# Hybrid encoder layer: the convolution group normalised two tiles a unit with its high parts on VectorE, and the values of two head pairs placed one unit later

## The chip, the cores and the metric

One core of a Trainium2 chip runs the whole program in one launch. The metric is the device time of one execution in microseconds (us). The kernel before takes 1961.98 us, the median of three runs (1961.77 to 1962.09).

## The reference

One encoder layer over 512 tokens of 2048 channels, in float32, cut here to what matters:

```python
xn = rms_norm(x, attn_norm_g)
u_val, u_gate, q, k, v = split(xn @ w_in)                  # 5 x 1024 columns
y_conv = silu(layer_norm(dwconv31(u_val * sigmoid(u_gate)) + b, ln_g, ln_b))   # group A
y_na   = neighbourhood_attention(q, k, v, rpb)             # group B: 16 heads of 64, 8 x 16 window
mixed  = concat(rms_norm(y_conv, conv_out_g), rms_norm(y_na, na_out_g))
x = x + mixed @ w_out
up = dwconv3(rms_norm(x, ffn_norm_g) @ w_up)               # 2 x 5632 columns
gate, val = split(up)
x = x + (silu(gate) * val) @ w_down
return rms_norm(x, final_norm_g)
```

The change touches the LayerNorm, swish and closing norm of group A, and the step of group B in which the softmaxed scores are multiplied by the values.

## The kernel before, in words

Channels lie on the 128 partitions, tokens on the free axis; a tile is 128 x 512. Float32 products are made from two parts: an operand is split into a rounded high part and a low part that is the rest, and a product is high by high, high by low and low by high. Weights come in units of 128 x 1024, each with one DMA on SyncE's queue (`raw`), one ScalarE copy that makes the high part (`whi`, line 129) and one VectorE subtraction that makes the low part (`wlo`, line 130). `group` (lines 146 to 149) spends 24 matmuls on one unit: 16 with the high part, then 8 with the low part. `AHEAD` has the parts of three later units made while a unit is multiplied; `whi` and `wlo` have four buffers each, so the parts of unit n+4 can be made once unit n has been multiplied.

The text counts these units from the start of the program. `ORDER` gives the order of the projections. For head pair p (1 to 7) the q projection takes units 44+4p and 45+4p, the k projection units 46+4p and 47+4p; pair 6 has units 68 to 71, pair 7 units 72 to 75. Units 76 to 91 are the half of the output projection that reads group A (`out_half(ma, read_a)`), units 92 to 107 the half that reads group B.

After the last matmul of each unit `tick` lets two lists of generators take one step each: `steps` holds `attention()` (later `norm_b()`), `asteps` holds `group_a()`. What a step traces on TensorE is kept behind that matmul; work of the other engines is only ordered by its place in the program, by data and by buffers. When a step of `attention` yields a true value, `group_a` is passed over in that unit. A planner turns the traced program into one fixed order for each engine. It gives earlier instructions precedence; `shifted` moves the place at which an instruction counts (the copies of line 597 count 100 places sooner).

`attention()` does for each head pair p: load the bias tables (line 628); one unit later the products with the values of pair p-1 (`values`, line 608) and the scores of pair p (`scores`, line 562), `taken` for pair p-1 and `softmax` for pair p; three units after that (four for p in `LATER`) the transposes of the softmaxed scores (`turn`, line 588) and their copies to SBUF (`turned_p`, line 597, tiles `pt`), which `values` reads. The matmuls of the values, the scores and the transposes are pinned to program order among themselves. `values` writes two PSUM banks: one of tag "po" and one of tag "mm", which has three banks and also holds the sums of `project`. Those leave the bank through VectorE's product with the inverse root (line 536), which is traced behind the tick of the projection's second unit.

`group_a()` starts when the taps of the depthwise convolution are done. Its eight tiles `ys` are centred and squared in one step (lines 508 to 510) and, after three units and the inverse root (`roots_of_sums`, lines 271 to 284), normalised in one step: for each tile a VectorE product with the root (line 517), a ScalarE Silu (line 518) and `split` (line 208) into `mah` and `mal`, a ScalarE copy (line 211) and a VectorE instruction (line 212). Eight squares (lines 217, 220) and seven additions (line 221) follow in the same step. `RA_AFTER` units later the second root is made: `halved` splits the sum on ScalarE and VectorE (lines 260, 261), and one unit later two matmuls (`column_sums`, line 268) add it over the partitions.

Counted out through the generators, the two lists do this in the units that matter (a step stands behind the matmuls of its unit):

| unit | steps before |
|---|---|
| 62 | A: mean; centre and square tiles 0 to 7 |
| 64 | transposes and copies of pair 3 |
| 65 | values 3, scores 4, softmax 4 |
| 66, 67 | A: halves of the sum; column sums, root, normalise and split tiles 0 to 7, squares |
| 68 | transposes and copies of pair 4 |
| 69 | values 4, scores 5, softmax 5 |
| 73 | transposes and copies of pair 5; A: halves |
| 74 | values 5, scores 6, softmax 6 |
| 75 | A: column sums, second root |
| 78, 79 | transposes of pair 6; values 6, scores 7, softmax 7 |
| 82, 83 | transposes of pair 7; values 7, halves of group B's sum |

Tiles of 128 x 512 in SBUF come from one pool of 75 (`t2`): the parts of x, `ma`, `mb`, q, k, the scores, `pt` and all that is passing.

Of the kernel before, what the change touches and what calls it, by code (L numbers as in the profile page):

```python
# [12 lines left out]
AF = mybir.ActivationFunctionType  # L13
ALU = mybir.AluOpType
# [17 lines left out]
NC_ = CONV // P  # L32
# [29 lines left out]
ROW = 2048  # L62
ORDER = "aaaaaaVVaqaqqqqqqq"
LATER = (5, 6)
RA_AFTER = 5

PCOLS = [("g1", KD), ("dww", NC_ * CK), ("dwb", NC_), ("lng", NC_), ("lnb", NC_), ("cog", NC_),
         ("nag", NC_), ("g2", KD), ("fww", 2 * NF * 3), ("fwb", 2 * NF)]
# [9 lines left out]
def layer(ctx: ExitStack, tc: tile.TileContext, xT, xg, xn, xw, w_0, w_in, w_v, w_out, w_up, w_down, par, tab, g3, out):  # L78
    nc = tc.nc
# [16 lines left out]
    def t2(name, dt=F32):  # L96
        return tp.tile([P, S], dt, tag="t2k", name=name)
# [8 lines left out]
    def pc(name, i):  # L106
        o = POFF[name] + i
        return prm[:, o:o + 1]
# [12 lines left out]
    def raw_unit(src, n):  # L121
        raw = t4([P, U * P], "raw")
        return raw, nc.sync.dma_start(raw[:, :n], src)
# [81 lines left out]
        if job:  # L205
            open_job.append(job)

    def split(src, g, name):

        h, l = t2(name + "h", F32R), t2(name + "l", F32R)  # L210
        nc.scalar.activation(h, src, AF.Copy, scale=g)
        nc.vector.scalar_tensor_tensor(l, src, g, h.bitcast(F32), op0=ALU.mult, op1=ALU.subtract)
        return h, l

# [99 lines left out]
    for k in range(ROWS):  # L314
# [9 lines left out]
        else:  # L324
            his = [t2("weh", F32R)[:, :P], t2("weh", F32R)[:, P:n]]
            h, l = t2("xh", F32R), t2("xl", F32R)
            g = both[:, S + n:S + n + 1]
# [21 lines left out]
    for u in range(2):  # L349
        raw, i = raw_unit(w_in[1, :, u * U * P:(u + 1) * U * P], U * P)  # L350
# [8 lines left out]
    for step in ORDER:  # L359
# [5 lines left out]
        i = next(a_ if step == "a" else q_)  # L365
# [63 lines left out]
    def grid(t):  # L429
        return t.rearrange("p (r g c) -> p g r c", g=NB, r=WH)  # L430
# [4 lines left out]
    ys, ypair, gate = [], [], []  # L435
# [55 lines left out]
    ma, ra = [], []  # L491

    def group_a():
        yield
        while taps:
            yield
        acc = t2("acc")
        nc.vector.tensor_add(acc, ys[0], ys[1])
        for i in range(2, NC_):
            nc.vector.tensor_add(acc, acc, ys[i])  # L500
        two = halved(acc)
        yield
        yield
        ps = column_sums(two)
        mu = t2("mu")
        nc.vector.tensor_scalar(mu, ps, 1.0 / CONV, None, op0=ALU.mult)
        acc = t2("acc")
        for i in range(NC_):
            nc.vector.tensor_sub(ys[i], ys[i], mu)
            sum_sq(acc, ys[i], i == 0)  # L510
        yield
        yield
        yield
        r = yield from roots_of_sums(acc, CONV, "rln")
        acc = t2("acc")
        for i in range(NC_):
            nc.vector.tensor_mul(ys[i], ys[i], r)
            nc.scalar.activation(ys[i], ys[i], AF.Silu, scale=pc("lng", i), bias=pc("lnb", i))  # L518
            ma.append(split(ys[i], pc("cog", i), "ma"))
        for i in range(NC_):  # L520
            sum_sq(acc, ys[i], i == 0)
        for _ in range(RA_AFTER):
            yield

        ra.append((yield from roots_of_sums(acc, CONV, "ra")))

# [15 lines left out]
    def attention():  # L542


        def banks(name):
            two = psa.tile([P, 2, S], F32, tag="sc", name=name)
            return [two[:, j, :2 * SLOTS] for j in range(2)] + [
                psa.tile([P, 2 * SLOTS], F32, tag="tr", name=name, bufs=2) for _ in range(2)]

        def scores(q, k, quad, both, more):  # L550
            todo = [[], []]
            for i, (odd, even) in enumerate(quad):
                if even:
                    todo[i] += [(odd, 0, odd - 1, 3), (even, 3, even - 1, 3)]
                else:
                    todo[i] += [(odd, 0, odd - 1, 2), (odd, 2, 0, 2), (even, 4, even, 2)]
            order = [(1, 0), (1, 1), (0, 0), (0, 1)] if len(todo[1]) > 2 else [(0, 0), (1, 0), (0, 1), (1, 1)]
            order += [(1, 2)] * (len(todo[1]) > 2)
            for i, n in order:
                b, to, g, w = todo[i][n]  # L560
                for j, hp in enumerate(hps):
                    m = nc.tensor.matmul(both[j][hps[i], to * DH:(to + w) * DH], q[hp, b * DH:(b + 1) * DH],  # L562
                                         k[hp, g * DH:(g + w) * DH], start=True, stop=True)
                    if more or (i, n, j) != (*order[0], 0):
                        pin(m)

        def softmax(both, tb):
            soft = []
            for j in range(2):
                flat = t2("s")[:, :2 * SLOTS]  # L570
                s = flat.rearrange("p (i k) -> p i k", i=2)
                nc.vector.scalar_tensor_tensor(flat, both[j], DH ** -0.5, tb[:, j], op0=ALU.mult, op1=ALU.add)
                nm = sm.tile([P, 2], F32, tag="nm", name="nm")
                nc.vector.tensor_reduce(nm, s, axis=AX.X, op=ALU.max, negate=True)
                su = sm.tile([P, 2], F32, tag="su", name="su")
                for i in range(2):
                    nc.scalar.activation(s[:, i], s[:, i], AF.Exp, bias=nm[:, i:i + 1], accum_out=su[:, i:i + 1])
                nc.vector.reciprocal(su, su)
                for i in range(2):
                    nc.scalar.activation(s[:, i], s[:, i], AF.Copy, scale=su[:, i:i + 1])  # L580
                soft.append(flat)
            return soft

        def turn(soft, four):
            for n, (s, ps) in enumerate(zip(soft, four)):
                ps = ps.rearrange("p (h c k) -> p c h k", h=2, c=3)
                for c in range(3):
                    m = nc.tensor.transpose(ps[:, c], s[:, c * P:(c + 1) * P], ident)  # L588
                    if n or c:
                        pin(m)  # L590

        def turned_p(four):
            pts = []
            for ps in four:
                pt = t2("pt")[:, :2 * SLOTS]
                with shifted(-SOONER):
                    i = nc.scalar.activation(pt, ps, AF.Copy)
                pts.append(pt)
            copies[:] = [i]
            return pts  # L600

        def values(p, pts, po):
            v = vs[2 * p // NP_]
            cols = [slice(at, at + DH) for at in (p % (NP_ // 2) * P + j * DH for j in range(2))]
            for n, slot in enumerate(TURNS):
                for i, (g, quad, at, w, b) in enumerate(slot):
                    for j in (1, 0):
                        m = nc.tensor.matmul(po[i][hps[j], b * DH:(b + w) * DH], v[g // 2][hps[i], cols[j]],  # L608
                                             pts[2 * quad + j][hps[i], at * DH:(at + w) * DH],
                                             start=n == 0, stop=n == len(TURNS) - 1, skip_group_check=True)  # L610
                        if (n, i, j) != (0, 0, 1):
                            pin(m)

        def taken(p, po):
            ao = t2("ao")
            nc.scalar.activation(grid(ao), blocks(po[0]), AF.Copy)
            nc.vector.tensor_add(grid(ao), grid(ao), blocks(po[1]))
            mb.append(split(ao, pc("nag", p), "mb"))
            sum_sq(acc_na, ao, p == 0)

        pts = None
        for p in range(NP_ + 1):
            while len(qks) < min(p + 1, NP_):
                yield
            if p < NP_:
                tabs = [t4([P, 2, 2 * SLOTS], "tab") for _ in QUADS]
                for n, tb in enumerate(tabs):
                    nc.sync.dma_start(tb, tab[2 * p:2 * p + 2, :, n * 2 * SLOTS:(n + 1) * 2 * SLOTS]
                                      .rearrange("h p k -> p h k"))
            yield  # L630
            if p:
                po = [psa.tile([P, S], F32, tag="po", name="po"), psm.tile([P, S], F32, tag="mm", name="po")]
                values(p - 1, pts, po)
            if p < NP_:
                four = banks("sc")
                for n, quad in enumerate(QUADS):
                    scores(*qks[p], quad, four[2 * n:][:2], p or n)
            if p:
                taken(p - 1, po)
            if p == NP_:  # L640
                return
            soft = [s for n in range(2) for s in softmax(four[2 * n:][:2], tabs[n])]
            for i in range(4 if p in LATER else 3):
                yield i == 0
            four = banks("trp")
            turn(soft, four)
            pts = turned_p(four)

    p, n = -1, 0
# [522 lines left out]
```

## Time and profile before

| what | before |
|---|---|
| median of three runs | 1961.98 us |
| the profiled execution's own time | 1962.36 us |
| its span in the profile | 1960.4 us |
| TensorE (PE) busy | 1938.6 us, 99% |
| VectorE (DVE) busy | 1611.0 us, 82% |
| ScalarE (ACT) busy | 1083.8 us, 55% |
| GpSimd (POOL) busy | 226.3 us, 12% |
| mean granted TensorE clock | 0.995 |

The busy times are of one profiled execution. Matmuls are pipelined, so a busy TensorE is one that always has a matmul under way. A row of the timeline gives the start, the length, the engine, the line, the operation, tile written and tiles read, how many instructions are merged, and in brackets the idle time of the engine before them with what ended it. The list of waits gives the total, the number and the longest.

### The profile page before, as it was taken

The numbers are of one execution on the slowest core, as the hardware profiler recorded it, in microseconds if no ns is written. First come the engines' busy times: TensorE is split into PE (matmuls) and PEld (weight loads), VectorE is DVE, ScalarE is ACT, GpSimd is POOL, SyncE is SP. The second block draws the span as 40 slices with busy tenths as digits, with TensorE's granted clock in tenths as the row PEclk, the third lists the DMA queues.
The fourth block names the chain that finished last, engine by engine and source line by source line (L and its number), as shares of the span: only waits on it lengthen the run. The fifth ranks groups of instructions, "written<-read, shape, count | busy, mean of one in ns | idle before, by whom it ended". The sixth has DMA issues, their size and how long they took to land.

```text
span 1960.4 us, 27992 instructions
## 1 busy us (share of the span) xinstructions
PE 1938.6 (99%) x10327; PEld 1652.5 (84%) x10327; DVE 1611.0 (82%) x2310; ACT 1083.8 (55%) x1725; POOL 226.3 (12%) x310
## 2 busy tenths in 40 slices
PE   9999999979999999999999999999999999999998
PEld 8888888868888888888888888888888888888886
DVE  5999878975657898888888888888889898885764
ACT  7222233576526666666666666666666644554654
POOL 0111111100011111111111111111110300000000
PEclk9999999999999999999999999999999999999999
DMA  9676667767758899999999999999995967666553
GB/s 372 179 194 178 190 182 189 194 167 218 251 151 215 212 250 253 270 243 271 241 270 244 270 247 265 262 249 263 249 257 166 386 239 236 216 215 194 192 201 121
DMA packets 141529, 448.89 MB, mean 229 GB/s; under 512 B 14928, under 2 KB 27216, under 8 KB 139984
## 3 DMA queue, kind: packets, MB, share of 16 engines
q1 hardware_dynamic: 89168, 291.90, 43.1%
q0 software_dynamic: 42624, 148.92, 35.1%
q10 hardware_dynamic: 9600, 6.29, 1.1%
q8 instruction: 81, 1.33, 0.3%
q14 instruction: 56, 0.46, 0.1%
HBM read 428.17 MB, written 111.15 MB: 275 GB/s over the span
## 4 chain that ended last, share of the span: by engine, by line
PE 97%; ACT 1%; DVE 1%; issue 0%; ACTq 0%
PE pu L823 44%; PE pd L962 21%; PE pj L146 5%; PE pj L147 5%; PE pj L149 5%; PE pv L417 4%; PE po L146 3%; PE po L147 3%; PE po L149 3%; PE pj L455 1%; PE po L608 1%; PE pj L459 1%; PE sc L562 1%; PE trp L588 0%; PE trx L718 0%; ACT y L518 0%
## 5 line engine op out<-in xcount | busy, mean ns | idle before, releaser
L129 ACT ACTIVATE whi<-raw 128x1024 fp32r<-128x1024 f32 (+1 forms) x574 | 604.1, 1055 | 550.6 <-PE pd L962 116.0
L130 DVE TENSOR_TENSOR wlo<-raw,whi 128x1024 fp32r<-128x1024 f32 (+1 forms) x574 | 698.6, 1218 | 214.8 <-ACT whi L129 186.5
L823 PE MATMUL pu<-xc,whi 128*128 128x512 f32 x2464 | 593.1, 391 | 0.0
L823 PEld LDWEIGHTS pu<-xc,whi 128*128 128x128 f32 x2464 | 451.4, 188 | 86.8 <-DVE xc L711 0.4
L823 PEld LDWEIGHTS pu<-xc,wlo 128*128 128x128 f32 x2464 | 319.4, 191 | 13.7
L823 PE MATMUL pu<-xc,wlo 128*128 128x256 f32 x2464 | 324.3, 283 | 0.0
L962 PE MATMUL pd<-whi,ho 128*128 128x512 f32 x1232 | 305.1, 389 | 0.0
L962 PEld LDWEIGHTS pd<-whi,ho 128*128 128x128 f32 x1232 | 231.1, 188 | 48.7 <-DVE vl L836 0.5
L146 PE MATMUL pj<-xh,whi 128*128 128x512 f32 x464 | 182.0, 392 | 0.0
L485 DVE SCALAR_TENSOR_TENSOR y<-ch,prm,y 128x500 f32<-128x500 f32 (+14 forms) x240 | 176.9, 741 | 5.4
L147 PE MATMUL pj<-xl,whi 128*128 128x512 f32 x464 | 180.6, 389 | 0.0
L962 PE MATMUL pd<-wlo,ho 128*128 128x512 f32 x616 | 165.1, 389 | 0.0
L962 PEld LDWEIGHTS pd<-wlo,ho 128*128 128x128 f32 x616 | 115.6, 188 | 24.0
L832 ACT ACTIVATE pu<-pu 128x512 f32<-128x512 f32 x132 | 76.6, 580 | 92.0 <-PE pu L823 92.0
L772 POOL DMA_DIRECT2D raw<-in_w_up x88 | 78.6, 893 | 351.5 <-DVE wlo L130 160.8
L203 POOL DMA_DIRECT2D ws<-in_w_down x88 | 79.9, 907 | 316.7 <-DMA ws<-in_w_down 126.5
L149 PE MATMUL pj<-xh,wlo 128*128 128x512 f32 x464 | 114.6, 389 | 0.0
L146 PEld LDWEIGHTS pj<-xh,whi 128*128 128x128 f32 x464 | 87.1, 188 | 19.5 <-issue 1.6
L149 PEld LDWEIGHTS pj<-xh,wlo 128*128 128x128 f32 x464 | 87.1, 188 | 18.1
L147 PEld LDWEIGHTS pj<-xl,whi 128*128 128x128 f32 x464 | 87.1, 188 | 17.8
L200 POOL DMA_DIRECT2D ws<-ws x44 | 23.3, 530 | 317.5 <-PE pj L149 102.9
L200 POOL DMA_DIRECT2D ws<-in_w_down x44 | 23.4, 531 | 298.5 <-PE pj L149 125.9
(215 smaller groups left out, 2109.2 us busy)
## 6 DMA issues: line engine op xcount, KB each, us to landing
raw<-in_w_up SPq DMA_DIRECT2D x220, 512.0 KB, 5.9
ws<-in_w_down POOLq DMA_DIRECT2D x132, 512.0 KB, 6.5
raw<-in_w_up POOLq DMA_DIRECT2D x88, 512.0 KB, 7.4
raw<-ws SPq DMA_DIRECT2D x88, 512.0 KB, 3.3
raw<-in_w_down SPq DMA_DIRECT2D x66, 512.0 KB, 3.8
raw<-in_w_in SPq DMA_DIRECT2D x58, 512.0 KB, 5.3
ws<-ws POOLq DMA_DIRECT2D x44, 512.0 KB, 5.5
raw<-in_w_out SPq DMA_DIRECT2D x32, 512.0 KB, 4.9
```

Source lines behind the costliest of these rows:

```text
L129: i = nc.scalar.activation(hi[:, :n], raw[:, :n], AF.Copy)
L130: j = nc.vector.tensor_sub(lo[:, :n], raw[:, :n], hi[:, :n].bitcast(F32))
L146: nc.tensor.matmul(ps, hi, mh, start=first and k == 0, stop=False)
L147: nc.tensor.matmul(ps, hi, ml, start=False, stop=False)
L149: i = nc.tensor.matmul(ps, lo[:, wk * P:(wk + 1) * P], mh, start=False, stop=last and k == len(ws) - 1)
L203: nc.gpsimd.dma_start(wsum[c][k], w_down[k, {1: A21, 2: A11, 4: A11, 6: A12}[c]], accum_op=ALU.add, max_dma_last_dim=ROW)
L417: m = nc.tensor.matmul(banks[c], xs[2 * u + k][x][:, c * P:(c + 1) * P], w[l][:, k * S:(k + 1) * S], start=u == x == l == k == 0, stop=las ...
L485: nc.vector.scalar_tensor_tensor(y[:, a:b], h[:, a + j - PAD:b + j - PAD], prm[:, o:o + 1], y[:, a:b], op0=ALU.mult, op1=ALU.add)
L772: nc.gpsimd.dma_start(a[c], w_up[f, q2], accum_op=ALU.add)
L823: i = nc.tensor.matmul(ps[:, :n], part[:, k * P:(k + 1) * P], comb[c][k][:, :n], start=j == 0 and not more, stop=j == 2 * U - 1, skip_grou ...
L832: nc.scalar.activation(to, ps, AF.Copy)
L962: m = nc.tensor.matmul(ps[i], h[:, o + t * P:o + (t + 1) * P], w[:, d], start=start and not more and kind == 0 and j == 0, stop=stop and k ...
```

## The change

`group_a` yields inside its two loops over the tiles. The centring takes three tiles in each of two units and two in the third; the unit in which the root is taken stays. The normalisation takes two tiles a unit, each with its square and its addition behind its split. The wait of `RA_AFTER` units is gone; the halves of the second sum come in the unit behind the last two tiles. `split` gets a switch, with which the high part is made by VectorE's tensor_scalar, and `group_a` sets it. `attention` yields once more ahead of the tables where pair p-1 is in `SLOW`, that is for p = 5 and 6.

```diff
-RA_AFTER = 5
+SLOW = (4, 5)
...
-    def split(src, g, name):
+    def split(src, g, name, vector=False):
 
         h, l = t2(name + "h", F32R), t2(name + "l", F32R)
-        nc.scalar.activation(h, src, AF.Copy, scale=g)
+        if vector:
+            nc.vector.tensor_scalar(h, src, g, None, op0=ALU.mult)
+        else:
+            nc.scalar.activation(h, src, AF.Copy, scale=g)
         nc.vector.scalar_tensor_tensor(l, src, g, h.bitcast(F32), op0=ALU.mult, op1=ALU.subtract)
...
             nc.vector.tensor_sub(ys[i], ys[i], mu)
             sum_sq(acc, ys[i], i == 0)
-        yield
-        yield
+            if i % 3 == 2:
+                yield
         yield
         r = yield from roots_of_sums(acc, CONV, "rln")
...
-            ma.append(split(ys[i], pc("cog", i), "ma"))
-        for i in range(NC_):
+            ma.append(split(ys[i], pc("cog", i), "ma", True))
             sum_sq(acc, ys[i], i == 0)
-        for _ in range(RA_AFTER):
-            yield
+            if i % 2 == 1:
+                yield
...
             while len(qks) < min(p + 1, NP_):
                 yield
+            if p - 1 in SLOW:
+                yield
             if p < NP_:
```

With the same counting, the units become:

| unit | steps after |
|---|---|
| 62, 63, 64 | A: centre and square tiles 0 to 2; 3 to 5; 6 and 7 |
| 66, 67 | A: halves; column sums, root, tiles 0 and 1 |
| 68 | transposes and copies of pair 4; A: tiles 2 and 3 |
| 69 | A: tiles 4 and 5 |
| 70 | values 4, scores 5, softmax 5 |
| 71, 72, 73 | A: tiles 6 and 7; halves; column sums, second root |
| 74 | transposes and copies of pair 5 |
| 76 | values 5, scores 6, softmax 6 |
| 80, 81 | transposes of pair 6; values 6, scores 7, softmax 7 |
| 84, 85 | transposes of pair 7; values 7, halves of group B's sum |

## The prediction

> **What bounds the kernel now.** I read the page first, then the list of waits for TensorE, then the stretches around the one long wait, then the timelines of three engines there. The page and the waits:
>
> ```profile
> span 1960.4 us, 27992 instructions
> PE 1938.6 (99%) x10327; PEld 1652.5 (84%) x10327; DVE 1611.0 (82%) x2310; ACT 1083.8 (55%) x1725; POOL 226.3 (12%) x310
> PE po L608 <- ACT pt L597: 12.7, 1, 12.7
> PE warm L117 <- DVE ones L112: 1.1, 1, 1.1
> ```
>
> TensorE sets the time from end to end: it is idle for 1960.4 - 1938.6 = 21.8 us, and 12.7 us of that is a single wait, of the values' matmuls for the copies of the turned scores. So work moved between other engines, or among steps, can gain only at that place; elsewhere it can only lose. The stretches (busy time of PE, PEld, DVE, ACT and POOL, then the granted clock, DMA) show what the wait does besides:
>
> ```profile
> 430.00:442.60 12.60, 0.00 (x0) 0.00 (x0) 10.25 (x16) 12.60 (x24) 0.00 (x0) 0.60 0.47 116
> 442.60:445.20 2.60, 2.59 (x52) 2.59 (x56) 2.50 (x4) 1.85 (x2) 0.00 (x0) 0.50 0.97 333
> 445.20:447.20 2.00, 2.00 (x41) 1.50 (x34) 1.51 (x2) 1.05 (x2) 0.00 (x0) 0.75 0.64 216
> 447.20:452.60 5.40, 5.40 (x24) 4.46 (x25) 4.73 (x9) 3.05 (x8) 0.00 (x0) 1.00 0.65 219
> ```
>
> ScalarE is busy through the whole wait. Behind it TensorE has a granted clock of 0.50, then 0.75, then 1.00 again. What that costs stands in the chain of waits: start, length, line, of an undisturbed pair of the same steps and of the pair behind the wait.
>
> ```profile
> 350.77 1.37 PE po L608 x38
> 352.15 1.36 PE sc L562 x31
> 442.61 2.62 PE po L608 x38
> 445.23 1.91 PE sc L562 x31
> ```
>
> 2.62 - 1.37 = 1.25 us and 1.91 - 1.36 = 0.55 us, 1.80 us together. The wait thus costs 12.70 + 1.80 = 14.50 us.
>
> Why were the copies late? TensorE's timeline (transposes of pair 4, last matmuls of unit 69, values 4) and ScalarE's and VectorE's groups between 425.5 and 447:
>
> ```profile
> 422.98 1.48 PE L588 MATMUL trp<-ident,s 128*128 128x128 f32 x12
> 427.94 1.98 PE L149 MATMUL pj<-xh,wlo 128*128 128x512 f32 x8
> 442.61 2.62 PE L608 MATMUL po<-pt,v 64*64 64x64 f32 x48 [12.70 <-ACT pt L597]
> ...
> L518 ACT ACTIVATE y<-y,prm 128x512 f32<-128x512 f32 x8 | 6.3, 801 | 0.9 <-DVE y L517 0.9
> L212 DVE SCALAR_TENSOR_TENSOR mal<-y,prm,mah 128x512 fp32r<-128x512 f32 x8 | 5.7, 746 | 1.7 <-ACT mah L211 1.7
> L211 ACT ACTIVATE mah<-y,prm 128x512 fp32r<-128x512 f32 x8 | 5.6, 706 | 0.0
> L517 DVE TENSOR_TENSOR y<-y,rln 128x512 f32<-128x512 f32 x8 | 4.9, 684 | 0.0
> L221 DVE TENSOR_TENSOR acc<-acc,sq 128x512 f32<-128x512 f32 x7 | 4.8, 690 | 0.8 <-ACT sq L220 0.2
> L220 ACT ACTIVATE sq<-y 128x512 f32<-128x512 f32 x7 | 3.7, 615 | 0.0
> L130 DVE TENSOR_TENSOR wlo<-raw,whi 128x1024 fp32r<-128x1024 f32 x2 | 2.4, 1218 | 0.0
> L597 ACT ACTIVATE pt<-trp 128x384 f32<-128x384 f32 x4 | 1.6, 472 | 0.0
> ```
>
> The transposes end near 424.2, yet the four copies stand in ScalarE's queue behind all 24 instructions of the normalisation, some 15 us of them. The planner's order explains it, I think, by the pool. The product for k of pair 5 (its projection ended at 417) and the copies come in this order:
>
> ```profile
> 412.17 0.68 DVE L536 TENSOR_TENSOR q<-pj,rstd 128x512 f32<-128x512 f32 x1
> 421.96 0.69 DVE L282 SCALAR_TENSOR_TENSOR r<-r,v 128x512 f32<-128x512 f32 x1 [1.36 <-ACT r L281]
> 437.33 3.73 ACT L220 ACTIVATE sq<-y 128x512 f32<-128x512 f32 x7
> 440.97 0.68 DVE L536 TENSOR_TENSOR k<-pj,rstd 128x512 f32<-128x512 f32 x1
> 440.97 1.59 ACT L597 ACTIVATE pt<-trp 128x384 f32<-128x384 f32 x4
> ```
>
> VectorE idles 1.36 us at 421 and does not take k's product, which was ready; it comes at the very moment at which the last square has been placed, and so do the copies. I read this as new tiles of the pool being handed out in program order: `pt` gets none until the squares of the whole step have theirs. The change cuts that step, so this holder is gone.
>
> **The change part by part.** *Later values.* Their place moves from behind unit 69 to behind unit 70. One unit is 5.44 us by two neighbours of the chain:
>
> ```profile
> 456.45 1.81 PE pj L149 x8
> 461.89 1.81 PE pj L149 x8
> ```
>
> TensorE goes on at 429.91 (442.61 - 12.70) with unit 70 and reaches values 4 at 435.35. *Fewer things ahead of the copies.* Ahead of `pt` in ScalarE's queue stand now at least two Silus and two squares, at most all eight Silus and two squares. From the first Silu at 426.25, by 0.71 a Silu (eight in 5.7 by spacing) and 0.52 a square (seven in 3.73), the copies start between 428.7 and 433.0, and end, with 1.6, by 434.6. That is 0.7 us or more before they are needed: the 12.70 us go, and with them the 1.80 us of clock.
>
> The Trainium skill ("TensorE: Matmul & The Clock Gate", Part 1) has it that about 3.4 us without work put the array at half clock, and that as long a busy stretch lifts it again. The rows of 0.50 and 0.75 agree; no run here shows an idle stretch between 1.1 and 12 us, so that a short new wait keeps full clock is the page's word alone.
>
> *High parts by VectorE.* Eight ScalarE copies of 0.61 (5.6 busy less overlap: 4.9 us) leave; eight VectorE instructions come. The trace has no tensor_scalar with this shape and rounded output; the nearest are, with float32 in and out,
>
> ```profile
> L483 DVE TENSOR_SCALAR y<-ch,prm 128x512 f32<-128x512 f32 x8 | 4.3, 541 | 0.0
> L1055 DVE TENSOR_SCALAR xr<-xr,rsy 128x512 f32<-128x512 f32 x6 | 2.8, 482 | 0.1
> ```
>
> I take 0.54, the one with an operation on a fresh tile, with 0.48 as the lower end: 3.8 to 4.3 us more on VectorE. This is what may come late next. VectorE was busy for 10.25 of the 12.60 us of the wait, and that wait no longer gives it time to catch up. Its queue from 425.53 to the product for q of pair 6 (behind unit 69's step): six products at 0.61, six high parts at 0.54, six low parts at 0.70 (four came in 2.78), five additions at 0.66, the product for k 0.68, two `wlo` at 1.2, the product for q 0.68: 3.7 + 3.2 + 4.2 + 3.3 + 0.7 + 2.4 + 0.7 = 18.2, so 443.7; with the products of the last two tiles drawn ahead 1.2 more. Unit 72 starts at 429.91 + 2 x 5.44 + 2.73 (values and scores) = 443.5 and needs a "mm" bank: of the three, k of pair 6 and values 4 hold two, so it waits for q's product. That is 0.2 to 1.4 us; with the lower price of the high parts nothing. I put 0.5 us into the sum. `wlo` of unit 73 lies behind that and isn't needed before 452: covered by three units of running ahead.
>
> *Column sums two units sooner.* The second root now runs behind unit 73 and not 75, four units behind the last tiles' step two earlier; in exchange the first output tile, behind unit 76, has its root at hand. It is hidden if the last two tiles are through by then, which the first rival doubts. *Centring in three parts:* the same instructions, the root in the same unit: nothing. *Pair 5 to 7 later by one or two units:* values 7 and group B's sum move from behind unit 83 to 85, and the root of B is needed from unit 92: nothing. The extra wait in `attention` stands ahead of the tables' DMA, so these go with it and SyncE's queue keeps its gap of one unit to their use.
>
> *Table loads.* Softmax 5 now lies between the Silus of tiles 4, 5 and 6, 7, unless these run ahead. A switch in the trace:
>
> ```profile
> 450.33 1.28 ACT L577 ACT_TABLE_LOAD   x1 [2.33 <-DVE nm L574]
> 451.62 0.46 ACT L577 ACTIVATE s<-s,nm 128x192 f32<-128x192 f32 x1
> 458.18 0.78 ACT L580 ACTIVATE s<-s,su 128x192 f32<-128x192 f32 x2
> ```
>
> One switch more costs 1.29 us of ScalarE, off the path: 0 in the sum.
>
> The Trainium skill ("ScalarE: Activation LUTs", What ACT_TABLE_LOAD costs) speaks against the change here: it puts a switch at 2.66 us with the drain. By the row the next activation starts 1.29 us after the load did; a drain ahead of it would lie in the 2.33 us that were idle anyway. By the page the sum stays, and the first rival's wait grows by an estimated 1.4 us.
>
> Sum: 1962.36 - 12.70 - 1.80 + 0.5 = 1948.4 for an execution like the profiled one, whose time lies 0.38 above the median: 1948.0.
>
> **The rivals.** *First: the wait moves to the column sums of the second root.* Behind unit 73, at 443.5 + 0.5 + 2 x 5.44 = 454.9, TensorE needs the halves of the sum. VectorE is at 443.7 when it turns to pair 4's output (three instructions, 2.0) and the scores; softmax 5 then takes what it took before, 451.62 to 458.96, that is 7.3, from about 447.1 + 1.3 for the load: 455.7. Behind it two squares (1.1), an addition and two halves (0.6 each): 458.6, or with table, Silus and VectorE's parts in line too 461.3. TensorE would wait 3.7 to 6.4 us, plus up to 1.80 of clock: 1951.7 to 1956.2. For it speaks that steps are cut finely now and nothing else separates tile 7 from its sum; against it, that these two matmuls aren't pinned and only have to lie behind unit 73, so that the planner can put them among the matmuls of unit 74, and that in the trace of before no sum of this kind was waited for.
>
> *Second, slower:* the same place, with Silu and Exp alternating in ScalarE's queue. Each return costs two loads, 2.57, and holds the exponentials, hence tile 7's square. The gain is used up when the halves end at 454.9 + 12.7 = 467.6; from 461.3 that takes three such returns (7.7: 469.0). Then 14.1 + 1.8 + 0.5 stand against 14.5: 1963.9 against the median's 1961.98, and with two more returns 1969. Against it: the trace shows one load for each stage.
>
> *Third: the copies stay late.* If the pool isn't what held them, the planner may put all Silus, high parts aside, and the squares of four or six tiles ahead: the copies end near 436.7, 1.3 us late: 1949.
>
> *Fourth: the change does nothing,* since the wait is on something that the trace doesn't name: 1962. The copies follow the squares without a gap, which leaves little for it.
>
> **How the numbers follow.** About 0.2%, 3.9 us, is what a measurement of this kernel can tell from no change. Forecast, with small waits up to 2 us: 0.74. Third: 0.04. First: 0.12. Second 0.06, of which 0.05 beyond 0.2% with the further returns or a wait I haven't seen. Fourth 0.04. Faster than 1958.1: 0.74 + 0.04 + 0.11 = 0.89; within: 0.06; slower 0.05. The range goes from 1946.8 (no wait at all gives 1947.5, and 0.7 for what the stretches round) to 1953.5, into the middle of the first rival.
>
> **What would show it.** Right: the list of waits has no 12.7 us at line 608; line 211 for `mah` is on VectorE, near 0.54 each; the granted clock is 1.00 from 430 to 480; the copies of pair 4 start before 434. The step on banks is right if a wait for VectorE's line 536 of 0.2 to 1.4 us stands ahead of unit 72. The first rival shows as a wait at line 268 for VectorE's line 261; the second as more than one Silu table load at line 518. Wrong altogether would be a wait of over 10 us anywhere in units 67 to 92, or one at line 608 again.

## The result and the profile after

| what | before | after |
|---|---|---|
| median of four runs | 1962.03 us | 1950.72 us |
| ratio of the runs, 95% interval | | 0.9941 (0.9924 to 0.9959) |
| the profiled execution's own time | 1962.36 us | 1950.75 us |
| its span | 1960.4 us | 1949.0 us |
| mean granted TensorE clock | 0.995 | 0.999 |

The changed kernel is 11.3 us faster by the medians; 1948.0 us was forecast, with 1946.8 to 1953.5 as the range. Lines behind 211 have moved in the changed kernel: the values are at line 610, the copies at 599, the column sums at 271, the product for q and k at 538, the high part at 212.

The page of after, and its list of waits for TensorE:

```profile
span 1949.0 us, 27983 instructions
PE 1937.8 (99%) x10327; PEld 1651.1 (85%) x10327; DVE 1613.1 (83%) x2318; ACT 1078.5 (55%) x1717; POOL 225.7 (12%) x310
PE warm L117 <- DVE ones L112: 1.1, 1, 1.1
PE pj L146 <- DVE q L538: 1.0, 1, 1.0
PE st L271 <- ACT ah L263: 0.6, 1, 0.6
```

The 12.7 us at the values have no row any more. Two small ones have come: at a projection for VectorE's product of q, and at the column sums for ScalarE's half. The timelines give the places (TensorE: values 4, unit 71's last matmuls, the first of unit 72, unit 72's last, unit 73's last, the column sums, transposes of pair 5; then ScalarE's copies of pair 4 and its half of the second sum, VectorE's product for k of pair 5, and the eight high parts on VectorE with shortest, median and longest duration):

```profile
435.76 1.44 PE L610 MATMUL po<-pt,v 64*64 64x64 f32 x48
442.25 1.97 PE L149 MATMUL pj<-xh,wlo 128*128 128x512 f32 x8
445.27 0.47 PE L146 MATMUL pj<-xh,whi 128*128 128x512 f32 x1 [1.04 <-DVE q L538]
449.02 1.98 PE L149 MATMUL pj<-xh,wlo 128*128 128x512 f32 x8
454.46 1.98 PE L149 MATMUL pj<-xh,wlo 128*128 128x512 f32 x8
460.43 0.50 PE L271 MATMUL st<-ah,ones 128*128 128x512 f32 x1 [0.59 <-ACT ah L263]
462.15 0.40 PE L271 MATMUL st<-al,ones 128*128 128x512 f32 x1
463.07 1.48 PE L590 MATMUL trp<-ident,s 128*128 128x128 f32 x12
431.32 1.59 ACT L599 ACTIVATE pt<-trp 128x384 f32<-128x384 f32 x4
459.76 0.61 ACT L263 ACTIVATE ah<-acc 128x512 fp32r<-128x512 f32 x1
432.34 0.68 DVE L538 TENSOR_TENSOR k<-pj,rstd 128x512 f32<-128x512 f32 x1
L212 DVE TENSOR_SCALAR mah<-y,prm x8: 466/478/486, 429.0 to 454.8; 128x512 fp32r<-128x512 f32 x8
```

The copies end at 432.9, and values 4 start 2.9 us later without a wait, in 1.44 us and not 2.62. From unit 71 to unit 72 the last matmuls are 6.77 us apart (442.25 to 449.02) where a unit is 5.44: 1.33 us lost at the bank, of which 1.04 is listed as a wait. From unit 73's last matmuls, which end at 456.27 (454.46 and the chain's 1.81), one unit and the 0.46 us of two column sums would lead to 462.17; the chain has the transposes at 463.24: 1.07 us lost at the column sums. They were put among the matmuls of unit 74, in two pieces.

The stretch with the wait at the bank keeps its clock (the column ahead of the last two), and so does the one with the column sums:

```profile
443.60:449.00 5.40, 4.36 (x19) 3.30 (x18) 4.61 (x9) 2.53 (x3) 0.00 (x0) 1.00 0.97 244
452.00:470.00 18.00, 17.41 (x83) 14.26 (x82) 12.24 (x22) 14.57 (x31) 2.30 (x3) 1.00 0.74 224
```

One more difference lies ahead of all of this. The chain's first product, and the timeline's last matmuls of the first unit behind the values' projection, each in the profile of before and then of after:

```profile
4.85 2.05 PE pj L455 x6
4.84 2.51 PE pj L458 x6
227.15 1.98 PE L149 MATMUL pj<-xh,wlo 128*128 128x512 f32 x8
227.63 1.98 PE L149 MATMUL pj<-xh,wlo 128*128 128x512 f32 x8
```

0.46 us, in code that the change doesn't touch; 0.48 us at the second place, and the same 0.48 at the last matmuls ahead of values 3 (401.56 and 402.04). With this the account of the two profiled executions closes: 14.50 recovered, less 1.33, 1.07 and 0.48, is 11.62; the times differ by 1962.36 - 1950.75 = 11.61. That it fits to a hundredth is luck: where the last long stretch of matmuls starts (1537.09 and 1525.27) the two are 11.82 us apart, and their spans differ by 11.4.

### The profile page after: what moved, and what is told of

It reads as the page before. It is cut to its first block, busy times and chain, and to the rows that moved or that the text cites. A ratio compares the mean times of both kernels' runs of the same rounds, so it can differ in the third digit from the quotient of the medians.

```text
span 1949.0 us, 27983 instructions
## 1 busy us (share of the span) xinstructions
PE 1937.8 (99%) x10327; PEld 1651.1 (85%) x10327; DVE 1613.1 (83%) x2318; ACT 1078.5 (55%) x1717; POOL 225.7 (12%) x310
## 3 DMA queue, kind: packets, MB, share of 16 engines
q8 instruction: 81, 1.33, 0.3%
## 4 chain that ended last, share of the span: by engine, by line
PE 96%; DVE 1%; ACT 1%; issue 0%; DMA 0%; ACTq 0%; DVEq 0%
PE pu L827 44%; PE pd L966 21%; PE pj L149 5%; PE pj L146 5%; PE pj L147 5%; PE pv L420 4%; PE po L146 3%; PE po L147 3%; PE po L149 3%; PE pj L458 1%; PE pj L462 1%; PE po L610 0%; PE trp L590 0%; PE sc L564 0%; PE trx L722 0%
```

## The experiments

Theory A is that of the prediction: the planner hands out the pool's tiles in program order, so the copies of pair 4 stood behind the squares of the whole normalisation. Against it stood that ScalarE is simply full (B), that the pool is (C), and that only some of the change's three parts matter. Times are medians; the ratio to the kernel before on the same chip is given with its interval.

**The copies in buffers of their own** (on the kernel before).

```diff
-NT = 75
+NT = 71
...
-                pt = t2("pt")[:, :2 * SLOTS]
+                pt = tp.tile([P, S], F32, tag="pt", name="pt", bufs=4)[:, :2 * SLOTS]
```

> The kernel before, with the copies of the turned scores in four buffers of their own and the pool of passing tiles cut from 75 to 71 (the same memory). Theory A (the planner hands out the pool's tiles in program order, so the copies get theirs only behind the eight squares): the copies of pair 4 stand ahead of the Silus, end near 426, the wait of 12.7 us at the values goes, 1947.9 to 1951 us, all without the change. Theory B (ScalarE is simply full there, whatever the order): the copies stay within 5 us of 441, 1957 us or more.

1966.31 us, ratio 1.0018 (1.001 to 1.0027). ScalarE's copies, TensorE's values and scores, VectorE's product for k:

```profile
423.95 1.61 ACT L597 ACTIVATE pt<-trp 128x384 f32<-128x384 f32 x4
429.85 1.44 PE L608 MATMUL po<-pt,v 64*64 64x64 f32 x48
444.52 2.91 PE L562 MATMUL sc<-k,q 64*64 64x192 f32 x36 [13.23 <-DVE k L536]
443.69 0.68 DVE L536 TENSOR_TENSOR k<-pj,rstd 128x512 f32<-128x512 f32 x1
```

Theory A holds for the copies: with tiles of their own they move 17 us forward, and the values start without a wait. B falls. But the time that was to follow doesn't come: it is 15 us above theory A's range. The scores of pair 5, which stand behind the values, wait 13.2 us for the product for k of pair 5. That product is itself traced behind the normalisation and ends at 444.4. In the kernel before, two waits lay on top of each other: the copies ended at 442.6, k's product at 441.65. The prediction saw k's product late and used it only as evidence for the order.

**A smaller pool** (on the kernel before), which takes the price of the 71 tiles out of the last run and tests C.

```diff
-NT = 75
+NT = 71
```

> The kernel before with a pool of 71 instead of 75 tiles and nothing else. Theory A (order of the hand-out, not the number): the wait at the values stays at 12.7 us, 1962 us within 1. Theory C (the pool is full there and the copies wait for a free tile): with four fewer the copies come later still, a wait of 14 us or more, 1963.5 us or more.

1967.18 us, ratio 1.002 (1.0011 to 1.0029).

```profile
PE po L608 <- ACT pt L597: 12.9, 1, 12.9
PE trx L718 <- DVE x L727: 3.5, 2, 1.8
```

The wait at the values is 12.9 for 12.7 us, so the number of tiles doesn't make it and C falls. The time lies in C's range all the same, and theory A's 1962 us is missed: the smaller pool costs elsewhere, with 3.5 us of new wait at the transposes of line 718 (1.4 us in the run above), and the slow clock behind the long wait costs 1.0 us more than before (0.8 in the run above). These are the larger part of the 4.3 and 3.5 us by which the two kernels with 71 tiles are slower than before; where the rest goes stays open.

**Only the later values** (on the kernel before, `RA_AFTER` kept).

```diff
+SLOW = (4, 5)
...
+            if p - 1 in SLOW:
+                yield
             if p < NP_:
```

> The kernel before, with the values of pairs 4 and 5 one unit later and nothing else of the change. Theory A: the copies stay behind the squares and end at 442.6, the values stand 5.4 us later in TensorE's order, so the wait shrinks to 7.3 us, the clock still falls, 1956.6 us. Rival (later values are what matters): no wait left, 1948 us.

1949.98 us, ratio 0.9934 (0.9921 to 0.9946): as good as the whole change. Theory A's number was wrong. TensorE, the last matmuls of units 69, 70 and 71 and values 4, then ScalarE's copies and the stretch around the wait:

```profile
428.20 1.98 PE L150 MATMUL pj<-xh,wlo 128*128 128x512 f32 x8
433.64 1.98 PE L150 MATMUL pj<-xh,wlo 128*128 128x512 f32 x8
439.08 1.98 PE L150 MATMUL pj<-xh,wlo 128*128 128x512 f32 x8
442.89 1.44 PE L609 MATMUL po<-pt,v 64*64 64x64 f32 x48 [1.84 <-ACT pt L598]
441.26 1.58 ACT L598 ACTIVATE pt<-trp 128x384 f32<-128x384 f32 x4
...
442.00:444.00 2.00, 1.11 (x45) 1.11 (x48) 1.90 (x4) 2.00 (x5) 0.00 (x0) 1.00 0.94 336
```

The copies are as late as before. But the planner put unit 71 ahead of the values too, so they moved by two units, 10.88 us: 12.70 - 10.88 = 1.82, and 1.84 was measured. And 1.84 us of waiting left the clock at 1.00, so its 1.80 us came back as well. That the order lets two units pass is shown; why isn't. A likely reason is in the code: behind unit 69 the values' second bank has its turn before unit 70's projection may take its own "mm" bank, while behind unit 70 the projection already has one and its second unit is free to go. It can't be the place alone: in the changed kernel, where the copies are early, the values at the same place let only unit 70 pass. No run changed any of this by itself.

**Only the high parts by VectorE** (on the kernel before).

```diff
-            ma.append(split(ys[i], pc("cog", i), "ma"))
+            ma.append(split(ys[i], pc("cog", i), "ma", True))
```

> The kernel before, with the eight high parts of the convolution group by VectorE and nothing else of the change. Theory A: ScalarE's queue ahead of the copies is shorter by eight copies of 0.61, 4.9 us, wait 7.8 us, 1957.1 us. Rival (VectorE holds the squares' tiles, since it now makes both parts): the copies come at 441 to 442 as before, 1962 us.

1961.25 us, ratio 0.9992 (0.9983 to 1.0001): no difference that this run can tell. The wait is 10.8 us, not 7.8. ScalarE:

```profile
438.40 1.22 ACT L600 ACTIVATE pt<-trp 128x384 f32<-128x384 f32 x3
440.71 0.49 ACT L600 ACTIVATE pt<-trp 128x384 f32<-128x384 f32 x1 [1.09 <-DVE acc L224]
```

Three copies do come earlier. The fourth waits for an addition of VectorE, which reads no score: I take it to be the release of a square's tile that the fourth copy inherits. VectorE, with the copies' work added, is then the later of the two. So the rival fits in its mechanism, as far as this reading goes, and was off in its size. That a wait 1.9 us shorter brings next to nothing is the clock: in this execution the slow matmuls behind the wait cost 3.0 us, where 1.80 was found before.

**Only the cut** (the changed kernel, high parts on ScalarE, values back in their unit).

```diff
-SLOW = (4, 5)
+SLOW = ()
...
-            ma.append(split(ys[i], pc("cog", i), "ma", True))
+            ma.append(split(ys[i], pc("cog", i), "ma"))
```

> The changed kernel, with the high parts back on ScalarE and the values of pairs 4 and 5 back in their unit: the step of the convolution group is cut, nothing else. Theory A: the copies stand behind two tiles' work and the Silus drawn ahead, end at 432.5 to 434, the wait is 2.6 to 4.1 us and the clock may fall a little, 1950.5 to 1953 us. Rival (the cut alone takes the whole wait): 1948 us.

1953.2 us, ratio 0.9952 (0.994 to 0.9965). TensorE's values 4:

```profile
432.83 2.62 PE L610 MATMUL po<-pt,v 64*64 64x64 f32 x48 [3.09 <-ACT pt L599]
```

The wait has shrunk to 3.09 us, in the span that theory A gave. The values behind it take 2.62 us, as in the kernel before: the clock falls, not a little but to half, and the time ends 0.2 us above theory A's range.

**The cut and the high parts** (the changed kernel, values back in their unit).

```diff
-SLOW = (4, 5)
+SLOW = ()
```

> The changed kernel, with the values of pairs 4 and 5 back in their unit. Theory A: the copies end at 432.4 as in the changed kernel less its later start, the values want them at 429.9, a wait of 2.5 us with the clock at full; the bank of pair 6's q is then in time, 1950.5 to 1952 us. Rival (one unit more is what the change lives on): 1956 us or more.

1952.43 us, ratio 0.9949 (0.9936 to 0.9961). The wait has the size that was expected, but the clock doesn't stay, and the time is 0.4 us above the range:

```profile
PE po L610 <- ACT pt L599: 2.6, 1, 2.6
...
432.67 2.50 PE L610 MATMUL po<-pt,v 64*64 64x64 f32 x48 [2.57 <-ACT pt L599]
...
430.00:432.00 2.00, 0.10 (x1) 0.00 (x0) 2.00 (x4) 2.00 (x5) 0.00 (x0) 1.00 1.07 169
432.00:434.00 2.00, 1.33 (x30) 1.33 (x34) 2.00 (x5) 2.00 (x5) 0.00 (x0) 0.72 0.84 179
434.00:436.00 2.00, 2.00 (x42) 1.83 (x36) 1.97 (x4) 2.00 (x4) 0.00 (x0) 0.50 0.55 184
436.00:438.00 2.00, 2.00 (x32) 1.59 (x25) 2.00 (x4) 2.00 (x4) 0.00 (x0) 0.93 0.29 41
```

2.57 us of idle time were enough for a granted clock of 0.50. The rival falls: without the extra unit the cut keeps most of the gain.

**The high parts back on ScalarE** (the changed kernel).

```diff
-            ma.append(split(ys[i], pc("cog", i), "ma", True))
+            ma.append(split(ys[i], pc("cog", i), "ma"))
```

> The changed kernel, with the high parts back on ScalarE. If VectorE's load makes the new wait of 1.04 us for q's bank, it goes (VectorE has 8 x 0.40 = 3.2 us less), and the wait at the column sums changes by under 1 us: 1949 to 1950 us. If ScalarE's load is what counts, the copies or the column sums come later by 1.2 us or more: 1951 us or more.

1948.63 us, ratio 0.9929 (0.9915 to 0.9942). The wait for q's product has no row any more; that at the column sums stays at 0.6. VectorE's product of q for pair 6, in the changed kernel and here:

```profile
444.44 0.68 DVE L538 TENSOR_TENSOR q<-pj,rstd 128x512 f32<-128x512 f32 x1
439.71 0.68 DVE L538 TENSOR_TENSOR q<-pj,rstd 128x512 f32<-128x512 f32 x1
```

It comes 4.7 us sooner, of which 0.8 is the earlier start of this execution. With the values later, moving the high parts to VectorE is the part that costs.

**The column sums one unit later** (the changed kernel).

```diff
-        ra.append((yield from roots_of_sums(acc, CONV, "ra")))
+        ra.append((yield from roots_of_sums(acc, CONV, "ra", 2)))
```

> The changed kernel, with the column sums of the second root one unit later. The 1.07 us that TensorE lost at them goes, 1949.7 us, if the halves of the sum were late by less than a unit; nothing, 1950.7 us, if those matmuls only filled a gap that the weights' parts would have left.

1948.94 us, ratio 0.9931 (0.9919 to 0.9944). The row for the column sums is gone; the one for q's product stays, at 1.2 us.

Three runs followed on one chip. **Both of the last two edits together:**

> The changed kernel, with the high parts back on ScalarE and the column sums of the second root one unit later. If the two losses of the changed kernel are separate (1.33 us at the bank of pair 6's q, 1.07 us at the column sums), both go: 2.4 us below the changed kernel on the same chip, near 1948.0 us. If one is only what shows when the other is gone, no better than either alone, 1948.6 to 1949 us.

1947.87 us, ratio 0.9924 (0.9912 to 0.9936), the fastest of all. Its whole list of waits for TensorE:

```profile
PE warm L117 <- DVE ones L112: 1.1, 1, 1.1
```

**Only pair 4 later** (the kernel before, `SLOW = (4,)`):

> The kernel before, with the values of pair 4 alone one unit later. If the gain comes from pair 4's values passing a unit of a projection that is under way, the same as with both pairs: 1949.5 to 1950.5 us. If pair 5's values need it too, a wait at the values of pair 5 and 1952 us or more.

1949.81 us, ratio 0.9937 (0.9924 to 0.9951), with the same wait of 1.84 us at values 4. In the kernel before, pair 5's part of `SLOW` isn't needed.

**The changed kernel again:**

> The changed kernel once more, beside the two others on the same chip: 1950.5 to 1950.9 us, with 1.0 us of wait for VectorE's product of q ahead of unit 72 and 0.6 us at the column sums.

1950.12 us, ratio 0.9937 (0.9924 to 0.9949), with 1.05 us and 0.60 us of wait at the two places, as expected. The fastest kernel lies 2.25 us below it, for 1.33 + 1.07 = 2.40 expected, and each edit took its own row out of the list of waits and left the other's: the two losses are separate. The 1950.12 us and the times of the two edits alone are 0.4 to 0.8 us below what was expected of them, which is no more than the start of an execution varies (last section).

## Why the prediction was right, and where it was off

*What bounds the kernel, and the 14.50 us.* Right. The wait and its clock came back whole, as the closed account shows, and the account has no gain anywhere else.

*Why the copies were late.* Right as to the order (own buffers move them, fewer tiles don't), incomplete as to what was late. The step "the change cuts that step, so this holder is gone" overlooked that k's product was held by the same order and would have stopped the scores 13.2 us. The cut frees both (k's product ends at 433.0 in the changed kernel, and the scores start at 437.0), and in the kernel with only the later values both are ready when they are wanted or shortly after. The forecast counted the wait once, for the copies, and came out because each of these parts happens to reach k's product too; that was luck.

*Later values.* The place behind unit 70 was right for the changed kernel: the copies, forecast to start between 428.7 and 433.0, start at 431.32 and are in time. What the delay is worth by itself was not seen: alone it brings what the whole change does, because it lets TensorE pass two units. The three parts don't add: later values alone 12 to 13 us, the cut alone 9, the high parts alone 1.6 or nothing, all together 11 to 12.5.

*High parts by VectorE.* The term was 0.5 us, from a span of 0 to 1.4 for the bank; it measured 1.33. The instruction itself cost what the cheaper of my two rows has, 0.478 us for 0.482; I had put in 0.54. What made the queue longer than the sum of 18.2 us (19.0 were measured, from 426.00 to 445.04) is in the order: all eight products with the root were drawn ahead of q's product, the case to which I had given 1.2 us more, and three `wlo` stood in front, not two.

*Column sums.* The first rival had the place right and the cost wrong: 1.07 us for 3.7 to 6.4. Its lateness was right: ScalarE's half ends at 460.37, 4.1 us behind unit 73. But, as the argument against it said, the two matmuls slid into unit 74; fifteen of that unit's matmuls went ahead of them, and the clock stayed. I gave the sum nothing for it, which is the second mis-sized term. Together the two terms are 2.40 us where 0.5 stood: 1.9 of the 2.7 us between forecast and median. Of the rest, 0.48 in the profiled executions is the start, and 0.35 is in the medians: the forecast took off the 0.38 us by which the profiled execution of before lay above its median, and that of after lies only 0.03 above its own.

*Table loads.* None was added: all Silus ran ahead of softmax 5, so there is one Silu load as before, and the second rival had no ground.

*Short waits keep the clock.* True here for 1.04 and 1.84 us, and false for 2.57 and 3.09 us. The trace of before could have told: its clock fell 2.65 us into the long wait (last section). The Trainium skill's figure ("TensorE: Matmul & The Clock Gate", Part 1) of about 3.4 us without work is more than that, and the measurement decides: a wait of 2.6 us has to be charged with slow matmuls behind it.

## What to carry to other kernels

When one wait holds the critical engine, list everything that the same cause makes late, not only what the wait names: the second in line sets what is left when the first is moved. Before spreading work over units, look whether the waiting step can simply come later, at a place where independent work is free to pass it; here that one yield was worth as much as the whole change. Work moved off a full engine should be priced in the queue that it joins, up to the next release that the critical engine wants from there.

## What the runs showed of the hardware

The granted clock fell to 0.50 with a wait of 2.57 us and stayed at 1.00 with waits of 1.04 to 1.84. Short windows that hold one change of the clock tell when it fell and rose: the kernel before, then only the cut, then the cut with the high parts.

```profile
432.50:433.00 0.50, 0.00 (x0) 0.00 (x0) 0.50 (x1) 0.50 (x2) 0.00 (x0) 0.56 1.10 201
446.00:446.50 0.50, 0.50 (x18) 0.45 (x14) 0.50 (x2) 0.00 (x0) 0.00 (x0) 0.78 0.95 238
...
432.00:432.50 0.50, 0.00 (x0) 0.00 (x0) 0.50 (x2) 0.50 (x3) 0.00 (x0) 0.59 1.17 213
438.50:439.00 0.50, 0.50 (x3) 0.35 (x3) 0.50 (x2) 0.50 (x2) 0.00 (x0) 0.58 0.79 166
...
432.50:433.00 0.50, 0.33 (x14) 0.33 (x18) 0.50 (x2) 0.50 (x2) 0.00 (x0) 0.88 0.88 156
436.00:436.50 0.50, 0.50 (x18) 0.43 (x14) 0.50 (x1) 0.50 (x2) 0.00 (x0) 0.71 0.00 0
```

A window of 0.50 us with a mean of 0.56 was at full clock for its first 0.06 us, so the clock fell at 432.56; the others read alike. It was at half from 432.56 to 446.22, from 432.09 to 438.92 and from 432.88 to 436.29: 13.66, 6.83 and 3.41 us, which is four, two and one times 3.41. The waits had begun at 429.91, 429.74 and 430.10, so it fell 2.65, 2.35 and 2.78 us into them, in the last case when the matmuls had just resumed. In the three other traces with a wait of over 10 us it fell 3.2 to 5.05 us in. What a fall costs is about half of the time that matmuls then run at half clock: 3.6, 6.1 and 3.4 us here, for 1.8, 2.9 and 1.7 us lost. So the wait of 3.09 us cost more behind it than the one of 12.70. The shortest wait that costs the clock isn't known from these runs; it need not be the same at every place.

The first products after the warm-up took 1.58 us in one execution and 2.65 in another of the same code, and this offset carried through: the profiled executions of the fastest kernel and of that with only the sums later, with identical work up to there, ended these products 1.12 us apart and reached later matmuls as far apart:

```profile
4.82 1.58 PE pj L458 x6
4.87 2.65 PE pj L458 x6
226.67 1.98 PE L149 MATMUL pj<-xh,wlo 128*128 128x512 f32 x8
227.79 1.98 PE L149 MATMUL pj<-xh,wlo 128*128 128x512 f32 x8
```

So a difference of about 1 us between two single executions says nothing of a change here. A tensor_scalar of 128x512 from float32 to the rounded type took 0.478 us on VectorE; the ScalarE copy that it replaced took 0.706.
